# Gated product kernel (x times y through tanh-GELU): two DRAM stretches in place of three, the first x load in four row groups

## The chip, the cores and the metric

The kernel runs on one core of a Trainium2 chip. The metric is the device time of one execution in microseconds; three runs of the kernel before gave a median of 119.74 us.

## The reference

```python
def setup_inputs():
    batch, dim = 1024, 4096
    return {
        "x": np.random.randn(batch, dim).astype(np.float32),
        "y": np.random.randn(batch, dim).astype(np.float32),
    }

def reference(x, y):
    z = x * y
    return (0.5 * z * (1 + np.tanh(np.sqrt(2 / np.pi) * (z + 0.044715 * z ** 3)))).astype(np.float32)
```

Everything is elementwise in float32. Each input and the output have 1024 x 4096 elements, 16.78 MB.

## The kernel before

Since nothing depends on an element's place, the kernel is free in how it lays the data out. It takes each array as one flat run of 128 x 32768 elements and cuts it into contiguous DRAM stretches (PIECES, L14). In each stretch, row p of 128 equal rows goes to SBUF partition p (`columns`, L51 to L55). The three stretches have rows of 1280, 16384 and 15104 elements, that is 5,120, 65,536 and 60,416 bytes. All of x (32768 columns, `xs`) stays in SBUF; the product and the GELU are written over it, and the stores read it. y goes through a smaller buffer, `ys`, of 20440 columns, so later parts of y overwrite earlier ones.

The work is ordered by hand:

- SP's queue (q1 in the profile) and ACT's queue (q10) both issue DMAs. `_hoist` (L25) moves an instruction to the program's very beginning, ahead of the opening barrier. The small x piece (on SP, L79) and the large second x piece (on ACT, L80) are hoisted.
- SP then waits for the small x piece (L81), loads y's first part (columns 1280 to 17664) and x's third piece (L82, L83). It loads y's other parts as the buffer comes free: the second after three products, the last, small one after four (Y_FREE, L18; loop L84 to L87).
- VectorE (DVE) multiplies in steps (STEPS, L20: four of 4096 columns, seven of 2048, one of 768, one of 1280), ahead of each part waiting for its x and y (L94, L95). ACT waits for each product (L105) and applies the GELU in place (L106). `sem_mul` and `sem_act` count products and activations.
- SP stores the three stretches (L111 to L115). The first store waits for y's second part to have landed (L113) besides its own activations; the small stretch is stored last. Then SP waits for the stores and clears the semaphores.

Each DMA adds 16 to its semaphore when all of it has landed. One row of a DMA is one packet in the trace; the core has 16 DMA engines, and a DMA of 128 rows gives each engine eight.

Of the kernel before, what the change touches and what calls it, by code (L numbers as in the profile page):

```python
# [1 line left out]

# [4 lines left out]


F32 = mybir.dt.float32
GELU = mybir.ActivationFunctionType.Gelu_apprx_tanh  # L10

PIECES = [(0, 1280), (1280, 17664), (17664, 32768)]  # L14

Y_LOADS = [(1280, 17664, 4056), (17664, 32768, 0), (0, 1280, 15104)]

Y_FREE = [0, 3, 4]  # L18

STEPS = [[4096] * 4, [2048] * 7 + [768], [1280]]  # L20
STORES = [(1280, 17664), (17664, 32768), (0, 1280)]
Y_BUF = 20440


def _hoist(nc, issued):  # L25

    here = nc.cur_bb.bb.instructions
    first = nc.main_func.blocks[0].instructions
    for ins in issued:
        del here[next(k for k, i in enumerate(here) if i is ins or i.name == ins.name)]  # L30
    engine = issued[0].engine
    at = next(
        k
        for k, i in enumerate(first)
        if i.engine == engine and type(i).__name__ == "InstDrain"
    )
    first[at:at] = issued


@with_exitstack  # L40
def kernel(
    ctx: ExitStack,
    tc: tile.TileContext,
    x: bass.AP,
    y: bass.AP,
    out: bass.AP,
):
    nc = tc.nc
    P = nc.NUM_PARTITIONS

    def columns(t, a, b):  # L51

        flat = t.flatten_outer_dims().rearrange("r c -> (r c)")
        pa, pb = next(q for q in PIECES if q[0] <= a and b <= q[1])
        return flat[P * pa : P * pb].rearrange("(p c) -> p c", p=P)[:, a - pa : b - pa]  # L55


    tc.close()
    tc.compile()  # L59

    xs = nc.alloc_sbuf_tensor("xs", [P, PIECES[-1][1]], F32).ap()
    ys = nc.alloc_sbuf_tensor("ys", [P, Y_BUF], F32).ap()
    sem_x = [nc.alloc_semaphore(f"sem_x{i}") for i in range(len(PIECES))]
    sem_y = [nc.alloc_semaphore(f"sem_y{i}") for i in range(len(Y_LOADS))]
    sem_mul = nc.alloc_semaphore("sem_mul")
    sem_act = nc.alloc_semaphore("sem_act")
    sem_o = [nc.alloc_semaphore(f"sem_o{i}") for i in range(len(STORES))]

    def load_x(i, engine=nc.sync):
        a, b = PIECES[i]  # L70
        return engine.dma_start(out=xs[:, a:b], in_=columns(x, a, b)).then_inc(sem_x[i], 16)

    def load_y(i):
        a, b, r = Y_LOADS[i]
        return nc.sync.dma_start(
            out=ys[:, r : r + b - a], in_=columns(y, a, b)
        ).then_inc(sem_y[i], 16)

    _hoist(nc, [load_x(0).ins])  # L79
    _hoist(nc, [load_x(1, nc.scalar).ins])  # L80
    nc.sync.wait_ge(sem_x[0], 16)  # L81
    load_y(0)  # L82
    load_x(2)  # L83
    for i in range(1, len(Y_LOADS)):  # L84
        if Y_FREE[i]:
            nc.sync.wait_ge(sem_mul, Y_FREE[i])
        load_y(i)  # L87

    n = 0
    done = {}  # L90
    for i, (a, b, r) in enumerate(Y_LOADS):
        for j, (xa, xb) in enumerate(PIECES):
            if xa <= a < xb:
                nc.vector.wait_ge(sem_x[j], 16)  # L94
        nc.vector.wait_ge(sem_y[i], 16)  # L95
        c = a
        for w in STEPS[i]:
            nc.vector.tensor_mul(  # L98
                out=xs[:, c : c + w],
                in0=xs[:, c : c + w],  # L100
                in1=ys[:, r + c - a : r + c - a + w],
            ).then_inc(sem_mul, 1)
            n += 1
            done[c + w] = n
            nc.scalar.wait_ge(sem_mul, n)  # L105
            nc.scalar.activation(  # L106
                out=xs[:, c : c + w], in_=xs[:, c : c + w], func=GELU
            ).then_inc(sem_act, 1)
            c += w

    for i, (a, b) in enumerate(STORES):  # L111
        if i == 0:
            nc.sync.wait_ge(sem_y[-2], 16)  # L113
        nc.sync.wait_ge(sem_act, done[b])
        nc.sync.dma_start(out=columns(out, a, b), in_=xs[:, a:b]).then_inc(sem_o[i], 16)  # L115
    for i in range(len(STORES) - 1):
        nc.sync.wait_ge(sem_o[i], 16)
    nums = sorted(s.num for s in [*sem_x, *sem_y, *sem_o[:-1], sem_mul, sem_act])
    assert nums == list(range(nums[0], nums[-1] + 1))
    nc.sync.sem_clear(range(nums[0], nums[-1] + 1))  # L120
    nc.sync.wait_ge(sem_o[-1], 16).then_inc(sem_o[-1], -16)


# [1 line left out]
_INS = ['x', 'y']  # L125
_OUTS = [((1024, 4096), 'float32')]


# [23 lines left out]
```

## Time and profile before

| | |
|---|---|
| runs, median (lowest, highest) | 119.74 us (119.72, 119.80) |
| span of the profiled execution | 118.52 us |
| the median less that span | 1.22 us |
| VectorE busy | 35.2 us (30%), 13 products |
| ScalarE (ACT) busy | 31.0 us (26%), 13 activations and a table load |
| HBM read, written | 33.55 MB, 16.78 MB |

The profiled execution has no time of its own beside its span; the 1.22 us are what the runs have around a span of this length. "Issue to landing" in the DMA table runs from the issuing instruction to the last arrival at the semaphore, so it holds the time that a transfer queued behind others. The strips divide the span, or the window asked for, into 40 equal slices; a digit is the busy share in tenths.

The SP queue issued its DMAs at 0.00 (small x), 13.57 (y, first part), 13.96 (x, third piece), 55.78 (y, second part), 60.12 (y, last part), 78.27, 96.55 and 97.71 us (the stores); ACT's queue issued its load at 0.13.

### The profile page before, as it was taken

What the parts mean: (1) busy time and instruction counts of PE and PEld (TensorE: products, weight loads), DVE (VectorE), ACT (ScalarE), POOL (GpSimd) and SP (SyncE); (2) the same over time, 40 slices, a digit from 0 to 9 for tenths busy, and PEclk for the clock granted to TensorE, in tenths of its full rate; (3) what the DMA queues carried; (4) which work ended last, traced back from release to release, by engine and by line L of the source; (5) the groups of instructions that cost most, each with busy time, mean ns of one, the idle gap of its engine ahead of it and who ended that gap; (6) DMA issues with size and microseconds to landing.
All of it is one profiled execution on the core that took longest, in us unless ns stands there. A gap on an engine that the chain in (4) does not pass through costs nothing.

```text
span 118.5 us, 82 instructions
## 1 busy us (share of the span) xinstructions
DVE 35.2 (30%) x13; ACT 31.0 (26%) x14; POOL 0.2 (0%) x4
## 2 busy tenths in 40 slices
DVE  0000000000000069999920000059999940000000
ACT  4000000000000000977975000006998990000000
POOL 0000000000000000000000000000000000000000
DMA  9888899889988897797797797798899887977975
GB/s 492 382 382 382 354 575 487 354 354 398 664 354 354 354 652 326 326 652 326 326 632 347 326 632 347 326 575 354 354 531 531 354 354 326 652 326 326 652 326 221
DMA packets 1296, 50.33 MB, mean 425 GB/s; under 512 B 144, under 2 KB 144, under 8 KB 528
## 3 DMA queue, kind: packets, MB, share of 16 engines
q1 hardware_dynamic: 1152, 41.94, 82.2%
q10 hardware_dynamic: 144, 8.39, 16.5%
HBM read 33.55 MB, written 16.78 MB: 425 GB/s over the span
## 4 chain that ended last, share of the span: by engine, by line
DMA 55%; DVE 24%; ACT 3%; issue 1%; DVEq 0%
DMA ys<-in_y_dram 43%; DVE xs L98 24%; DMA xs<-in_x_dram 11%; ACT xs L106 3%; DVEq L95 0%
## 5 line engine op out<-in xcount | busy, mean ns | idle before, releaser
L98 DVE TENSOR_TENSOR xs<-xs,ys 128x2048 f32<-128x2048 f32 (+3 forms) x13 | 35.2, 2777 | 60.9 <-DMA ys<-in_y_dram 60.9
L106 ACT ACTIVATE xs<-xs 128x2048 f32<-128x2048 f32 (+3 forms) x13 | 29.7, 2301 | 65.1 <-DVE xs L98 65.1
L106 ACT ACT_TABLE_LOAD x1 | 1.3, 1283 | 1.6 <-PEq L59 1.6
L136 POOL MEMSET const-bfloat16-1.0<- 128x1 bf16 x1 | 0.1, 103 | 0.0
L136 POOL MEMSET const-uint8-127<- 128x1 uint8 x1 | 0.1, 102 | 0.0
L136 POOL MEMSET const-float32-0.0<- 128x1 f32 x1 | 0.1, 100 | 0.2 <-issue 0.2
L136 POOL MEMSET const-float32-1.0<- 128x1 f32 x1 | 0.1, 99 | 0.0
## 6 DMA issues: line engine op xcount, KB each, us to landing
xs<-in_x_dram SPq DMA_DIRECT2D x1, 7552.0 KB, 46.5
ys<-in_y_dram SPq DMA_DIRECT2D x1, 7552.0 KB, 22.5
out_dram<-xs SPq DMA_DIRECT2D x1, 7552.0 KB, 20.4
xs<-in_x_dram SPq DMA_DIRECT2D x1, 640.0 KB, 13.6
ys<-in_y_dram SPq DMA_DIRECT2D x1, 640.0 KB, 19.7
out_dram<-xs SPq DMA_DIRECT2D x1, 640.0 KB, 20.8
xs<-in_x_dram ACTq DMA_DIRECT2D x1, 30.4
ys<-in_y_dram SPq DMA_DIRECT2D x1, 29.0
```

What stands on the lines that cost most here:

```text
L98: nc.vector.tensor_mul(out=xs[:, c : c + w], in0=xs[:, c : c + w], in1=ys[:, r + c - a : r + c - a + w],).then_inc(sem_mul, 1)
L106: nc.scalar.activation(out=xs[:, c : c + w], in_=xs[:, c : c + w], func=GELU).then_inc(sem_act, 1)
L136: nc = _bacc.Bacc("TRN2", target_bir_lowering=False, num_devices=1)
```

## The change

There are two stretches (HALVES) of 15872 and 16896 elements a row, 63,488 and 67,584 bytes. The small piece is gone.

- x's first stretch is loaded by four DMAs of 32 rows each: group g takes partitions g, g + 4, g + 8 and so on. All add to one semaphore, and VectorE waits for 64 on it. Group 0 is hoisted on SP. The other groups and x's whole second stretch follow on SP with no wait between them. The rows of the second stretch are longer than 64 KB and are issued as 128 x 2 x 8448 elements.
- The hoisted DMA on ACT's queue is now y's first part (15872 columns) instead of x's large piece.
- y's second stretch is loaded in two parts of 12800 and 4096 columns, 51,200 and 16,384 bytes of each row, after three and after four products.
- Products and activations have new steps: three of 4096 and one of 3584 columns; five of 2048 and one of 2560; then 2048, 1280 and 768.
- There are two stores. The first waits for the four activations of its stretch and for the fifth product, which is the first on y's second part; the second waits for all activations.

```diff
-PIECES = [(0, 1280), (1280, 17664), (17664, 32768)]
+HALF = 15872
+HALVES = [(0, HALF), (HALF, 32768)]
 
-Y_LOADS = [(1280, 17664, 4056), (17664, 32768, 0), (0, 1280, 15104)]
+GROUPS = 4
 
-Y_FREE = [0, 3, 4]
-
-STEPS = [[4096] * 4, [2048] * 7 + [768], [1280]]
-STORES = [(1280, 17664), (17664, 32768), (0, 1280)]
+Y_LOADS = [(0, 15872, 4568, 0), (15872, 28672, 0, 3), (28672, 32768, 12800, 4)]
+STEPS = [[4096] * 3 + [3584], [2048] * 5 + [2560], [2048, 1280, 768]]
 Y_BUF = 20440
...
-    def load_x(i, engine=nc.sync):
-        a, b = PIECES[i]
-        return engine.dma_start(out=xs[:, a:b], in_=columns(x, a, b)).then_inc(sem_x[i], 16)
+    def load_group(g):
+        return nc.sync.dma_start(
+            out=xs[g::GROUPS, :HALF], in_=columns(x, 0, HALF)[g::GROUPS]
+        ).then_inc(sem_x[0], 16)
...
-    _hoist(nc, [load_x(0).ins])
-    _hoist(nc, [load_x(1, nc.scalar).ins])
-    nc.sync.wait_ge(sem_x[0], 16)
-    load_y(0)
-    load_x(2)
+    _hoist(nc, [load_group(0).ins])
+    _hoist(nc, [load_y(0, nc.scalar).ins])
+    for g in range(1, GROUPS):
+        load_group(g)
+    a, b = HALVES[1]
+    nc.sync.dma_start(out=xs[:, a:b], in_=columns(x, a, b)).then_inc(sem_x[1], 16)
     for i in range(1, len(Y_LOADS)):
-        if Y_FREE[i]:
-            nc.sync.wait_ge(sem_mul, Y_FREE[i])
+        nc.sync.wait_ge(sem_mul, Y_LOADS[i][3])
         load_y(i)
...
-    for i, (a, b) in enumerate(STORES):
-        if i == 0:
-            nc.sync.wait_ge(sem_y[-2], 16)
-        nc.sync.wait_ge(sem_act, done[b])
+    first = len(STEPS[0])
+    nc.sync.wait_ge(sem_act, first)
+    nc.sync.wait_ge(sem_mul, first + 1)
+    for i, done in enumerate((first, n)):
+        a, b = HALVES[i]
+        nc.sync.wait_ge(sem_act, done)
         nc.sync.dma_start(out=columns(out, a, b), in_=xs[:, a:b]).then_inc(sem_o[i], 16)
```

More of the change, by code (lines that the diff above doesn't have):

```diff
@@ L53, in columns @@
         flat = t.flatten_outer_dims().rearrange("r c -> (r c)")
-        pa, pb = next(q for q in PIECES if q[0] <= a and b <= q[1])
-        return flat[P * pa : P * pb].rearrange("(p c) -> p c", p=P)[:, a - pa : b - pa]
+        ha, hb = next(h for h in HALVES if h[0] <= a and b <= h[1])
+        return flat[P * ha : P * hb].rearrange("(p c) -> p c", p=P)[:, a - ha : b - ha]
     tc.close()
     tc.compile()
-    xs = nc.alloc_sbuf_tensor("xs", [P, PIECES[-1][1]], F32).ap()
+    xs = nc.alloc_sbuf_tensor("xs", [P, HALVES[-1][1]], F32).ap()
     ys = nc.alloc_sbuf_tensor("ys", [P, Y_BUF], F32).ap()
-    sem_x = [nc.alloc_semaphore(f"sem_x{i}") for i in range(len(PIECES))]
+    sem_x = [nc.alloc_semaphore(f"sem_x{i}") for i in range(2)]
     sem_y = [nc.alloc_semaphore(f"sem_y{i}") for i in range(len(Y_LOADS))]
@@ L66, with load_y @@
     sem_act = nc.alloc_semaphore("sem_act")
-    sem_o = [nc.alloc_semaphore(f"sem_o{i}") for i in range(len(STORES))]
-    def load_x(i, engine=nc.sync):
-        a, b = PIECES[i]
-        return engine.dma_start(out=xs[:, a:b], in_=columns(x, a, b)).then_inc(sem_x[i], 16)
-    def load_y(i):
-        a, b, r = Y_LOADS[i]
-        return nc.sync.dma_start(
+    sem_o = [nc.alloc_semaphore(f"sem_o{i}") for i in range(2)]
+    def load_group(g):
+        return nc.sync.dma_start(
+            out=xs[g::GROUPS, :HALF], in_=columns(x, 0, HALF)[g::GROUPS]
+        ).then_inc(sem_x[0], 16)
+    def load_y(i, engine=nc.sync):
+        a, b, r, _ = Y_LOADS[i]
+        return engine.dma_start(
             out=ys[:, r : r + b - a], in_=columns(y, a, b)
         ).then_inc(sem_y[i], 16)
-    _hoist(nc, [load_x(0).ins])
-    _hoist(nc, [load_x(1, nc.scalar).ins])
-    nc.sync.wait_ge(sem_x[0], 16)
-    load_y(0)
-    load_x(2)
+    _hoist(nc, [load_group(0).ins])
[4 more added lines that the diff above has]
+    nc.sync.dma_start(out=xs[:, a:b], in_=columns(x, a, b)).then_inc(sem_x[1], 16)
     for i in range(1, len(Y_LOADS)):
-        if Y_FREE[i]:
-            nc.sync.wait_ge(sem_mul, Y_FREE[i])
+        nc.sync.wait_ge(sem_mul, Y_LOADS[i][3])
         load_y(i)
     n = 0
[L90 to L94, printed above, removed]
+    for i, (a, b, r, _) in enumerate(Y_LOADS):
+        if i == 0:
+            nc.vector.wait_ge(sem_x[0], 16 * GROUPS)
+        if i == 1:
+            nc.vector.wait_ge(sem_x[1], 16)
         nc.vector.wait_ge(sem_y[i], 16)
@@ L103 @@
             n += 1
-            done[c + w] = n
             nc.scalar.wait_ge(sem_mul, n)
@@ L109 @@
             c += w
-    for i, (a, b) in enumerate(STORES):
-        if i == 0:
-            nc.sync.wait_ge(sem_y[-2], 16)
-        nc.sync.wait_ge(sem_act, done[b])
+    first = len(STEPS[0])
[4 more added lines that the diff above has]
+        nc.sync.wait_ge(sem_act, done)
         nc.sync.dma_start(out=columns(out, a, b), in_=xs[:, a:b]).then_inc(sem_o[i], 16)
-    for i in range(len(STORES) - 1):
-        nc.sync.wait_ge(sem_o[i], 16)
-    nums = sorted(s.num for s in [*sem_x, *sem_y, *sem_o[:-1], sem_mul, sem_act])
+    nc.sync.wait_ge(sem_o[0], 16)
+    nums = sorted(s.num for s in [*sem_x, *sem_y, sem_o[0], sem_mul, sem_act])
     assert nums == list(range(nums[0], nums[-1] + 1))
     nc.sync.sem_clear(range(nums[0], nums[-1] + 1))
-    nc.sync.wait_ge(sem_o[-1], 16).then_inc(sem_o[-1], -16)
+    nc.sync.wait_ge(sem_o[1], 16).then_inc(sem_o[1], -16)
 _INS = ['x', 'y']
```

## The prediction

> **What bounds the kernel now.** Read first: the page's strip and queue table; then the chain of waits; then the DMA view in narrow windows; last the trace's records of single DMA packets (one for each row that a DMA engine moves).
>
> ```profile
> span 118.5 us, 82 instructions
> ...
> DMA  9888899889988897797797797798899887977975
> ...
> q1 hardware_dynamic: 1152, 41.94, 82.2%
> q10 hardware_dynamic: 144, 8.39, 16.5%
> HBM read 33.55 MB, written 16.78 MB: 425 GB/s over the span
> ```
>
> The packets fill 82.2 + 16.5 = 98.7% of the sixteen engines' span. Idle are 1.3% of 118.5, about 1.5 us, and 1.0 of these lies ahead of the first packet. The chain of waits seems to say something else:
>
> ```profile
> 13.57 28.99 DMA ys<-in_y_dram
> ...
> 42.66 13.11 DVE xs L98 x3
> ...
> 55.78 22.47 DMA ys<-in_y_dram
> ...
> 80.56 13.30 DVE xs L98 x6
> ```
>
> It gives VectorE 13 us from 42.66. But it only follows semaphores back: the y load issued at 55.78 queued behind an x load that landed later:
>
> ```profile
> xs<-in_x_dram SPq DMA_DIRECT2D x1, 7552.0 KB, 46.5
> ys<-in_y_dram SPq DMA_DIRECT2D x1, 7552.0 KB, 22.5
> out_dram<-xs SPq DMA_DIRECT2D x1, 7552.0 KB, 20.4
> xs<-in_x_dram SPq DMA_DIRECT2D x1, 640.0 KB, 13.6
> ys<-in_y_dram SPq DMA_DIRECT2D x1, 640.0 KB, 19.7
> out_dram<-xs SPq DMA_DIRECT2D x1, 640.0 KB, 20.8
> ```
>
> That x load was issued at 13.96 and landed at 13.96 + 46.5 = 60.4. The y load behind it landed at 55.78 + 22.5 = 78.25. So the queue held work all the time, and compute is hidden. The same rows give the pace: an engine moved 8 rows of 60,416 B in 78.25 - 60.4 = 17.84 us, or 36.9 ps per byte; the small store's rows took (118.49 - 116.98)/8 = 0.189 us for 5,120 B, also 36.9. Time is bytes, plus what is lost at the start and in gaps. Two windows show those losses (40 slices each, 0.0 to 4.0 and 78 to 80 us; a packet is booked in the slice in which it starts, so zeros after the long rows have started are no idleness):
>
> ```profile
> DMA  0000000000995375796979799990000000000000
> ```
>
> ```profile
> DMA  9974997799499749950752999909000000000000
> ```
>
> In the first, nothing moves for 1.0 us, then 5 KB rows come in unevenly. In the second, the digits 0, 7, 5, 2 between 78.9 and 79.1 are engines that have finished the last y rows while the store's first rows, issued at 78.27, start at 79.11.
>
> **The change part by part.** Every byte still moves once. Per engine: before, 48 loaded and 24 stored rows; after, loads are 8 (x groups) + 8 (y) + 16 (x's second stretch, each row in two pieces of 33,792 B) + 8 + 8 = 48, stores 8 + 16 = 24. Bytes and row count equal: 0. Bounds: no row of 33,792 B is in this trace. The 5,120 B stores have packet starts 196.6 ns apart where 36.95 ps per byte make 189, 7 ns more. If the half rows alone cost that: 32 x 7 ns = 0.22 less the 0.06 of the 8 small stores given up, +0.17. If only the small ones cost it, -0.06. I take 0, being nearer to 60,416 B rows, which keep to the pace.
>
> *Start.* On average the engines are done with what x's first two pieces and y's first load hold (8 x 5,120 + 16 x 65,536 B, 40.18 us at 36.87 ps) at 41.87, a loss of 1.69. Following the packet records engine by engine splits it: the first packets begin between 1.01 and 1.61, mean 1.20; slow 5 KB rows cost 24 x (0.210 - 0.196) = 0.34 an engine, of which 0.23 are first rows (mean excess, the worst 0.756 against 0.196); the first 64 KB rows of ACT's queue cost 8 x (2.438 - 2.418) = 0.16. After, the hoisted DMA has 32 rows instead of 128, two for each engine if they spread evenly. With a quarter of the rows I give the ramp a quarter of its 0.6 us: mean start 1.08. First-row delay (0.23) and ACT queue's (0.16) stay, the 0.11 of later small rows goes: 1.47, so -0.22. Bounds: no delay beyond 1.01 at all, -0.68; each engine with the worst first row (+0.56), the worst ACT row (2.682 against 2.418, +0.26) and today's mean start: 2.02, +0.33. I take -0.22, since it keeps each row that has a counterpart.
>
> SP issues five more DMAs in a row (three groups, x's second stretch; the wait for x's first piece at L81 is gone), 0.4 us each as at L71: from about 1.6 to 3.2. The first group's two rows alternate with y's rows and last four times 2.34 us, to 10.4: cover 7 us. Without it, each late issue would cost its 0.4.
>
> *Middle.* x's first half and y's first load are 16 rows of 63,488 B; against before that is 73,728 B less, 2.72 us, and 0.22 of start: landed at 42.56 - 2.94 = 39.6. Three products of 4096 columns (13.1) let SP pass its wait at 52.8 for y's second part; the fourth (3.8) at 56.6 for the third. Behind these waits in SP's queue stand only the later y load and the stores. x's second stretch streams until 39.6 + 16 x 1.247 = 59.55, so y's second part is 59.55 - 52.8 - 0.85 = 5.9 us early (0.85: the store's issue at 78.27 to first packet 79.11). No gap. Were it later than that, every microsecond would count in full.
>
> *The gap at 79.* Mean end of the last y rows 79.08 by the records, mean first store packet 79.19: 0.11 lost, up to 0.31 on single engines. After, y's second part lands at 59.55 + 8 x 51,200 x 36.9 ps = 74.66; one product (2.29 + 0.1) and the issue pass to 77.05; store rows are ready at 77.9. The 16 KB rows of y last until 74.3 + 4.84 = 79.15 on the latest engine and 78.6 on the earliest, so they cover the new wait on the fifth product by 0.7. The gap closes: -0.11 (0 if the late engines set the end anyway; -0.31 if the most delayed does). If that cover were gone, each microsecond by which the product is late would stand in the span.
>
> *End.* The remaining products (four of 2.22, then 2.75, 2.22, 1.41, 0.87 by 1.05 ns a column) end at 93.2, the last ACTIVATE (0.83) at 94.1. The second store is ready by 95, the first streams to about 97.9: hidden by 3 us. One store less and one load semaphore more are single 9 ns packets: 0.
>
> Sum: 118.52 - 0.22 - 0.11 = 118.19. Runs have a median of 119.74, 1.22 above the profiled span; I keep that: 119.41, so 119.4.
>
> One rule stands against it. Every DMA of before has 128 rows; none shows 32. The Trainium skill, "DMA: Bandwidth & Descriptors", "Rules for kernel authors", says that peak rate wants 128 partitions in a DMA and that one 128-partition transfer beats split ones. "SBUF — State Buffer", section on the DMA port swizzle, explains it by ports, four neighbouring partitions to a port and the same port again 32 further on; rows 0, 4, 8 and so on reach all sixteen, but which engine gets which row no page says for 32 rows. If two engines met at one port and shared its rate, x's rows would take twice as long and the sum would be 138; if not, it stays 119.4.
>
> **The rivals.**
>
> *The start pays the same.* Lost time at the start could be latency that a long first row pays like a short one, and a start near 1.2. For it: 0.23 are first rows, and 64 KB rows are slow at first too. Against it: 0.6 us of ramp under 128 rows. Then only the gap is gained, or not even that: 119.6 to 119.7, no difference.
>
> *The row groups run slower.* Place: the first 39 us, where an engine moves 8 x rows of 2.34 us = 18.7. For it: no 32-row DMA is in the trace, and its slowest kind of row, 5,120 B, was 7% over its own best on average (0.210 for 0.196). Against: long rows keep 2.42 in either queue. At 7%: 119.74 + 1.31 - 0.33 = 120.7; at twice the time, the far end, 138. It decides from 0.33/18.7 = 1.8%, and from 3.0% it is a measurable loss.
>
> *The half rows are slow.* x's second stretch and the second store are 32 packets of 33,792 B in 40 us. Priced as the 5,120 B stores are (196.6 ns, 38.4 ps a byte), they cost 32 x 33,792 x 1.5 ps = 1.6 more: 119.4 + 1.6 = 121.0. Against it: the 7 ns look like a price per row, not per byte.
>
> *The change misses its cover.* The fifth product comes after y's last rows are through; it has 0.7 us to spare, and the product would have to be later by more. At 1 us late the gap is 0.3 and the time 119.7; at 1.5 us late, 120.2.
>
> **How the numbers follow.** About 0.2%, 0.24 us, is what a measurement of this kernel can tell from no change: below 119.50 is faster, above 119.98 slower. Forecast 0.47; equal start 0.22 (same); row groups 0.19; half rows 0.09; missed cover 0.03, counted half as same, half as slower. Faster 0.47, same 0.23, slower 0.30. The forecast's own terms reach from 119.74 - 0.68 - 0.31 - 0.06 = 118.7 to 119.74 + 0.33 + 0.17 = 120.2; both low ends together are unlikely, so I cut the range at 118.9, and carry it up to 120.8 over the 7% case. Left out are the half rows at full price and heavier group losses, about 0.17, and little below.
>
> **What would show it.** Right: sixteen engines' first packets within 0.2 us after 1.0; x rows of 2.34 us in all groups; first x and y landed by 39.6; no thin slices between 78 and 80; last landing near 118.1. Wrong: x rows in the groups above 2.40 us, half rows above 1.26, a thin strip before 39 or around 59, SP still issuing the groups when an engine runs dry, or VectorE's fifth product later than 78.

## The result and the profile after

The changed kernel takes 120.33 us (four runs, 120.23 to 120.69) against 119.73 for the kernel before in the same comparison (119.71 to 119.80). The ratio is 1.0052, interval 1.0039 to 1.0066: half a per cent slower, where the forecast was 0.3 per cent faster. The profiled execution took 120.37 us with a span of 119.02, so 1.35 lie around the span. (A second profile of the kernel before, further down, has 119.89 and 118.56, so 1.33. The 1.22 of the prediction set one run's span against other runs' median.)

The page of the changed kernel: span, strip, queues, and DMAs from issue to landing.

```profile
span 119.0 us, 81 instructions
...
DMA  9799779978987899998989696997997799898994
...
q1 hardware_dynamic: 1168, 42.21, 82.1%
q10 hardware_dynamic: 144, 8.13, 16.3%
HBM read 33.55 MB, written 16.78 MB: 423 GB/s over the span
...
xs<-in_x_dram SPq DMA_DIRECT2D x1, 8448.0 KB, 56.7
out_dram<-xs SPq DMA_DIRECT2D x1, 8448.0 KB, 23.5
xs<-in_x_dram SPq DMA_DIRECT2D x4, 1984.0 KB, 28.9
ys<-in_y_dram ACTq DMA_DIRECT2D x1, 7936.0 KB, 35.5
```

The kernel is as DMA-bound as before: the two queues' packets fill 82.1 + 16.3 = 98.4% of the engines' span. So the loss must be a matter of tenths in one place, and the narrow windows find it. First the DMA view from 0.0 to 4.0 us in slices of 0.1 us (a packet is booked where it starts):

```profile
DMA  0000000000099999000000000000000000000009
GB/s 0 0 0 0 0 0 0 0 0 0 0 3809 1905 1270 1905 1270 0 0 0 0 0 0 0 0 0 0 0 0 0 0 0 0 0 0 0 0 0 0 0 635
DMA packets 17, 1.08 MB, mean 270 GB/s; under 512 B 0, under 2 KB 0, under 8 KB 0
```

Sixteen rows start between 1.1 and 1.6 us, all 63,488 B long and all of ACT's queue, which this view lists alone with 16 packets. Only one more row starts before 4.0, though such a row takes 2.34 us and the next should have started from 3.5 on. Then the timeline of the first stretch:

```profile
0.00 0.54 SPq L67 DMA_DIRECT2D xs<-in_x_dram  x1
0.12 0.38 ACTq L73 DMA_DIRECT2D ys<-in_y_dram  x1
```

The 32-row DMA holds SP for 0.54 us, the 128-row one holds ACT for 0.38: y's rows came first, x's group second. And the DMA view from 78 to 80 us:

```profile
DMA  9977077797077909077099090999990999000900
```

Here rows of y and, from 79.1, of the store start at scattered times, so single zeros are no idleness; the packet records show no engine idle for more than 0.01 us there. The gap has closed as forecast.

**Where the loss sits.** The packet records give for each DMA the sixteen small packets with which the engines report its end. I took the latest of the sixteen engines at two points. "Start's loss": when it has moved the first x and y loads, less its bytes at 36.87 ps each. "Rest": from there, with the start's bytes put back, to its last packet. Before: 42.19 - 40.17 = 2.02, and 118.11 - 2.02 = 116.09; after: 39.96 - 37.45 = 2.51.

```
                                            first-row excess  start's loss  rest     end
kernel before                               0.23              2.02          116.09   118.11
kernel before, second profile               0.19              2.05          116.11   118.16
changed kernel                              0.65              2.51          116.06   118.57
```

"First-row excess" is how much longer an engine's very first row took than a later one of its size, mean of sixteen; times in us. The rest agrees within 0.05 us although it holds all the half rows, the new waits, the closed gap and one store less. The start costs 0.49 us more, and the end comes 0.46 later: the whole difference is there when the first x and y have landed. On average over the sixteen engines the start's loss is 1.70 before, as the prediction had it, and 2.02 after.

### The profile page after: what moved, and what is told of

Read it like the earlier page. It is cut to its first block, busy times and chain, and to the rows that moved or that the text cites. A ratio compares the mean times of both kernels' runs of the same rounds, so it can differ in the third digit from the quotient of the medians.

```text
span 119.0 us, 81 instructions
## 1 busy us (share of the span) xinstructions
DVE 35.2 (30%) x13; ACT 30.9 (26%) x14; POOL 0.2 (0%) x4
## 3 DMA queue, kind: packets, MB, share of 16 engines
q1 hardware_dynamic: 1168, 42.21, 82.1%
q10 hardware_dynamic: 144, 8.13, 16.3%
## 4 chain that ended last, share of the span: by engine, by line
DMA 50%; DVE 23%; ACT 5%; SPq 1%; issue 0%; DVEq 0%
DMA xs<-in_x_dram 31%; DVE xs L96 23%; DMA ys<-in_y_dram 18%; ACT xs L103 5%; SPq L67 1%; DVEq L93 0%
## 5 line engine op out<-in xcount | busy, mean ns | idle before, releaser
L96 DVE TENSOR_TENSOR xs<-xs,ys 128x2048 f32<-128x2048 f32 (+5 forms) x13 | 35.2, 2779 | 58.7 <-DMA xs<-in_x_dram 40.3
L103 ACT ACTIVATE xs<-xs 128x2048 f32<-128x2048 f32 (+5 forms) x13 | 29.6, 2302 | 62.7 <-DVE xs L96 62.7
## 6 DMA issues: line engine op xcount, KB each, us to landing
ys<-in_y_dram SPq DMA_DIRECT2D x1, 2048.0 KB, 23.1
```

The lines of the kernel that those rows point to most:

```text
L96: nc.vector.tensor_mul(out=xs[:, c : c + w], in0=xs[:, c : c + w], in1=ys[:, r + c - a : r + c - a + w],).then_inc(sem_mul, 1)
L103: nc.scalar.activation(out=xs[:, c : c + w], in_=xs[:, c : c + w], func=GELU).then_inc(sem_act, 1)
```

## The experiments

Each ratio is against the kernel before in the same comparison (119.82 to 119.91 us there).

**The start, first round.** Four edits of the changed kernel.

One DMA of 128 rows in place of the groups:

```diff
-GROUPS = 4
+GROUPS = 1
```

> x's first stretch in one hoisted DMA of 128 rows instead of four of 32; all else as in the changed kernel. In its profile the sixteen engines begin with y rows of ACT's queue (1.13 to 1.59 us) and each engine's first 63,488 B row takes 2.95 us on average where a later one takes 2.34, an excess of 0.61. Theory A (the strided 32-row DMA takes longer to be set up, 0.54 us at its issue against 0.38, so x comes second and the start is late): SP's x rows begin at about 1.0 again, first-row excess about 0.25, time 119.7 to 119.9. Theory B (any long row that is the first on its engine pays, whichever queue it is from): first-row excess 0.5 to 0.7 again, time 120.2 to 120.4.

120.45 us, ratio 1.0043 (1.0031 to 1.0055). Its DMA view from 0.0 to 4.0 us:

```profile
DMA  0000000009999900999000000000000000000009
GB/s 0 0 0 0 0 0 0 0 0 635 4444 1905 635 635 0 0 635 635 635 0 0 0 0 0 0 0 0 0 0 0 0 0 0 0 0 0 0 0 0 635
```

x's rows begin at 1.0, as theory A wants, and still take 3.09 us as first rows, an excess of 0.75. A is wrong: neither the groups nor the order of the queues is the cause. B had the mechanism, with excess and time slightly above its ranges. (For the changed kernel the records give 2.99 and an excess of 0.65, not the 2.95 and 0.61 of the expectation.)

Columns instead of rows, the hoisted DMA with 5,120 B rows that begin 63,488 B apart:

```diff
-GROUPS = 4
+GROUPS = 2
+CUTS = [0, 1280, HALF]
...
-            out=xs[g::GROUPS, :HALF], in_=columns(x, 0, HALF)[g::GROUPS]
+            out=xs[:, CUTS[g] : CUTS[g + 1]], in_=columns(x, CUTS[g], CUTS[g + 1])
```

> x's first stretch split by columns instead of by rows: the hoisted DMA takes 128 rows of 5,120 B, the next the other 58,368 B of each row. Both A and B: the start is that of the kernel before (first packets from 1.0, mean loss at the start 1.7 instead of 1.98, latest engine 0.49 earlier), time 119.7 to 119.9. If instead the loss comes from the two stretches, the half rows or the new waits, it stays at 120.2 to 120.4.

120.28 us, ratio 1.0032 (1.0020 to 1.0044): between the two cases. The profile, of the fastest of its runs (120.06 us), has a start's loss of 2.15 and a rest of 116.11. Its 5 KB first rows paid 0.53 us, twice as much as in the kernel before, where they lie end to end.

SP waiting for group 0 ahead of the other groups, and ACT's load not hoisted:

```diff
+    nc.sync.wait_ge(sem_x[0], 16)
     for g in range(1, GROUPS):
```

> SP waits for group 0 to have landed (about 14 us) ahead of the other three groups and x's second stretch, as the kernel before waited for its small piece. Theory C (the four DMAs that SP issues from 1.8 to 4.2 us, while the first rows are under way, slow those): first-row excess falls from 0.61 to 0.3 or less, time 119.8 to 120.0. Theories A and B: excess stays at about 0.6, time 120.2 to 120.5. The y rows cover the wait in every theory.

```diff
-    _hoist(nc, [load_y(0, nc.scalar).ins])
+    load_y(0, nc.scalar)
```

> y's first load is issued on ACT behind the opening barrier (about 1.8 us) instead of ahead of it, so the engines must begin with group 0 of x. Theory A: the group's rows begin late (1.3 us or more) though nothing is ahead of them, first-row excess about 0.25. Theory B: they begin at about 1.0 to 1.2 and pay 0.5 to 0.7. Time in A 120.0 to 120.4, in B 120.1 to 120.4; here the first packets decide, not the time.

The first took 120.66 us (1.0063, 1.0049 to 1.0076) with an excess of 0.70, a little above the range given: DMAs issued meanwhile do not slow the first rows, and theory C is wrong. The second took 120.75 us (1.0073, 1.0061 to 1.0085), more than either theory gave. With nothing ahead of it, the group's first packets come at 1.33 us or later, as A said of the set-up, but the excess is 0.80, even above B's 0.5 to 0.7. The strided 32-row DMA is slow to start; in the changed kernel y's rows, from 1.13 us on, fill the engines meanwhile.

**Place in DRAM, the gap, the second half.** The kernel before with the first piece inside a longer stretch:

```diff
+DRAM = [(0, 17664), (17664, 32768)]
...
-        pa, pb = next(q for q in PIECES if q[0] <= a and b <= q[1])
+        pa, pb = next(q for q in DRAM if q[0] <= a and b <= q[1])
```

> The kernel before with one thing changed: its small first piece lies inside a stretch of 17664 columns, so the hoisted DMA reads its 5,120 B rows 70,656 B apart instead of end to end. All DMAs keep their sizes and order. Theory D (rows that begin far apart in DRAM cost the first packets more: in the run by columns the same 5 KB rows, 63,488 B apart, paid 0.53 us as first packets and 0.67 an engine in all, against 0.23 and 0.34 in the kernel before): first-row excess about 0.5, latest engine 0.2 to 0.4 later, time 0.2 to 0.4 above before. Theory B (only the length of the first row counts): as before within 0.1.

120.13 us, ratio 1.0021 (1.0013 to 1.0030), excess 0.51, start's loss 2.21, rest 116.12. So a start with 5 KB rows that lie apart cost 0.2 us more than one with rows end to end. The edit did a little more than its expectation says: x's large piece, y's first and last parts and two of the stores lie at the wider pitch too. But the rest is as before, so nothing behind the start paid for it; which of the first loads' pitches counts is not separated.

The kernel before without the wait that makes its gap:

```diff
-        if i == 0:
-            nc.sync.wait_ge(sem_y[-2], 16)
```

> The kernel before without the wait for y's landing ahead of the first store (L113), so the store's rows stand behind y's last rows early and the gap at 79 us closes. If the gap costs the end what the prediction gave it: 0.1 us less than before. Theory S (the latest engine has no gap and alone sets the end; the gap only lets the early ones fall back): the latest engine's end unchanged, spread of the engines at the end 0.5 instead of 0.17 us, time as before within 0.05.

Neither: 121.04 us, ratio 1.0096 (1.0083 to 1.0109). The start is as before (1.98), the rest 117.16. Where y's last 5 KB rows should be through by 79.1, the DMA view from 78 to 80 us is thin to its end:

```profile
DMA  9592909626699098699929299589590429793499
DMA packets 94, 0.48 MB, mean 241 GB/s; under 512 B 0, under 2 KB 0, under 8 KB 94
```

Hardly an engine is idle, but 241 GB/s: the small rows took 2.5 us instead of 1.5, with the store's rows waiting behind them. The run can't say what the gap costs, because the early store costs ten times as much. An answer comes from the rest in profiles whose later rows ran at pace: 116.09, 116.11 and 116.12 with the gap, 116.06, 116.11 and 116.11 without (changed kernel, one group, columns). These kernels differ in more than the gap, but to the engine that ends last it is worth 0.05 us at most.

The changed kernel with the kernel before's hoisted DMA (a contiguous stretch of its own for 1280 columns, with a load of y and a store of its own):

```diff
+CUT = 1280
+DRAM = [(0, CUT), (CUT, HALF), (HALF, 32768)]
...
-GROUPS = 4
+GROUPS = 2
...
-            out=xs[g::GROUPS, :HALF], in_=columns(x, 0, HALF)[g::GROUPS]
+            out=xs[:, DRAM[g][0] : DRAM[g][1]], in_=columns(x, *DRAM[g])
```

> The changed kernel with x's first 1280 columns (and y's and the output's) in a contiguous stretch of their own: the hoisted DMA is that of the kernel before, the row groups are gone, and all from x's second stretch on is as changed; y's small piece is a load of its own on SP behind x's. Theories B and D: start as in the kernel before, time 0.0 to 0.15 above before. If something behind the start costs (half rows, the second y parts, the waits): 0.4 to 0.6 above before, as the changed kernel.

120.28 us, ratio 1.0033 (1.0020 to 1.0045): not the 0.0 to 0.15 expected. Excess 0.27, as in the kernel before, but a start's loss of 2.46 on the latest engine, much of it one engine whose first long row took 0.63 us too long, and a rest of 116.18. On average over the engines the start's loss is 1.81, near the kernel before's 1.70. It moves 96 rows an engine instead of 72, 24 of them small; eight of these lie in the rest, and at the prediction's 7 ns each that is an estimated 0.06 of the 0.1 there.

Rows of 1,280 B in the run by columns (`CUTS = [0, 320, HALF]`):

> The run by columns with a hoisted DMA of 320 columns: 128 rows of 1,280 B, 63,488 B apart. Theory D: first-row excess still about 0.5, time as in the run by columns or above (0.3 to 0.5 over before). Theory B: excess clearly smaller than 0.5, and y's long rows, which then start while the chip is still cold, pay instead; time 0.2 to 0.5 over before.

120.54 us, 0.63 above before and so above both forecasts; ratio 1.0052 (1.0039 to 1.0066), start's loss 2.72. The very first rows paid 0.16 on average, but later ones of the small rows up to 1.16: each engine met several delays. Shorter rows alone do not help; B as "length only" is too simple.

**Which array, which wait.** The kernel before with ACT's and SP's first large loads exchanged:

```diff
-    _hoist(nc, [load_x(1, nc.scalar).ins])
+    _hoist(nc, [load_y(0, nc.scalar).ins])
...
-    load_y(0)
+    load_x(1)
```

> The kernel before with ACT's hoisted load and SP's later one exchanged: ACT loads y's first part, SP x's large piece, sizes unchanged. Theory T (two arrays cold at once cost the start more than one): latest engine 0.2 to 0.4 later, time 0.2 to 0.4 above before. Otherwise within 0.1 of before.

119.90 us, ratio 1.0006 (0.9998 to 1.0015). Two arrays at once cost nothing: theory T is wrong. (Its profile is of the slowest of its runs, 120.39 us.) The like exchange in the run with a stretch of its own:

> The run with a stretch of its own for the first 1280 columns (0.37 above before), with the same exchange the other way round: ACT loads the rest of x's first half, SP the rest of y's. Theory T: its loss goes, time 0.0 to 0.15 above before. Theory W (what is missing is the kernel before's wait on SP, which keeps further DMAs from being issued into the start): stays at 0.3 to 0.4.

120.18 us, ratio 1.0031 (1.0019 to 1.0043), start's loss 2.22 (1.78 on average), rest 116.40. It stays slow, which W allowed, but W falls with the next run, the kernel before without SP's first wait:

```diff
-    nc.sync.wait_ge(sem_x[0], 16)
```

> The kernel before without SP's wait for the small piece (L81), so that y's first part and x's third piece are issued from about 1.6 us. Theory W: time 0.2 to 0.5 above before, with the loss in the first 5 us. Theory T: within 0.1.

119.91 us, ratio 1.0005 (0.9996 to 1.0014), start's loss 2.14, rest 116.14: no difference.

A small piece of 2560 columns in the kernel before (PIECES cut at 2560 and 18944, y's parts and steps to match):

> The kernel before with a small piece of 2560 columns: hoisted rows of 10,240 B end to end, and 3 us of y's last rows to cover the first store's issue. Theory S: the gap at 79 closes, which is worth nothing to the latest engine. Theories B and D: the start as before or a little later (longer first rows, 1.3 MB touched instead of 0.65): time 0.0 to 0.2 above before. If the gap counted: 0.1 below.

120.43 us, ratio 1.0055 (1.0043 to 1.0067): 0.57 above before, where 0.0 to 0.2 was the most expected. Its 10 KB first rows paid 0.61 us, almost as much as long ones, but the engines that started first paid it and those that started late did not: these rows all ended between 2.06 and 2.35 us, and the start's loss is 1.98. So it is the latest engine's sum that counts, not the first rows' mean. The gap closed, and the rest is 116.72. The time went in the middle: y's second part was issued at 57.30, the loads ahead of it ended at 59.9, and y's first rows behind them were 0.15 to 0.32 us too long on eight engines; one engine lost 0.5 in these rows. A lead of 2.6 us did not keep the rows at pace; 3.9 us in the kernel before (55.78 to 59.7) did. That is read from one profile, not tried.

**Regions, and the start alone.** A kernel before whose long rows begin half a 64 KB off (first piece 1344 columns), and one whose second piece has 15872 columns (in both, y's parts, steps and stores are changed to match):

```diff
-PIECES = [(0, 1280), (1280, 17664), (17664, 32768)]
+PIECES = [(0, 1344), (1344, 17728), (17728, 32768)]
```

> The kernel before with a small piece of 1344 columns: the 65,536 B rows behind it keep their length but begin 688,128 B into the array, 10.5 times 65,536, instead of 655,360, ten times. Theory P (the first touch of each 64 KB region costs a delay, and a row that straddles two pays twice): latest engine 0.2 to 0.4 later at the start, time 0.2 to 0.4 above before. If P is wrong: within 0.1.

```diff
-PIECES = [(0, 1280), (1280, 17664), (17664, 32768)]
+PIECES = [(0, 1280), (1280, 17152), (17152, 32768)]
```

> The kernel before with its second piece of 15872 columns, so that ACT's first rows are 63,488 B as in the changed kernel; small piece, waits and gap unchanged. Theory P: 0.2 to 0.4 above before. If only the length and order of the first rows count: within 0.1.

119.87 us (1.0007, 0.9998 to 1.0015) and 119.92 us (1.0007, 0.9998 to 1.0015), start's losses 1.99 and 1.96. Theory P is wrong, and 62 KB rows are as good as 64 KB ones behind short rows. The changed kernel with stretches of 16384 columns (y's parts and steps to match) agrees:

```diff
-HALF = 15872
+HALF = 16384
```

> The changed kernel with both stretches of 16384 columns: rows of exactly 65,536 B at multiples of 65,536, row groups kept. Theory P: first rows' mean excess falls from 0.65 to 0.45 or less, time 0.2 to 0.4 above before instead of 0.6. If P is wrong: excess 0.6 to 0.8, time 0.5 to 0.7 above before.

120.34 us, ratio 1.0045 (1.0029 to 1.0061), excess 0.71, start's loss 2.41. This run has no half rows either, as x's second stretch moves in rows of 65,536 B, and it is still slow. And the second profile of the kernel before:

> The kernel before, unchanged: a second profile of it. If the start's loss is a property of the kernel, its latest engine is again 1.9 to 2.2 us behind its bytes at the end of the first loads and the span again 116.1 more than that; if one lucky profile stood in the comparison, it is 2.4 or more.

119.85 us, ratio 0.9996 (0.9986 to 1.0006); its row is in the table above. The small loss at the start is no luck of one profile.

The kernel before with long rows first, its small piece no longer hoisted:

```diff
-    _hoist(nc, [load_x(0).ins])
+    load_x(0)
```

> The kernel before with its small piece no longer hoisted, so that the engines' first rows are ACT's 65,536 B rows; small piece, sizes, gap and tail stay. Theory B (an engine whose first row is long loses its whole first delay, and the engines lose unequally): first-row excess 0.6 to 0.8, latest engine 0.4 to 0.6 later, time 0.4 to 0.6 above before, with nothing of the changed kernel's second half in it. If the change's second half is what costs: within 0.1 of before.

122.83 us, ratio 1.0246 (1.0232 to 1.0260), far more than expected, because the edit did two things. The excess of the first rows is 0.72, as B said, with none of the change's second half there. When both hoisted loads were in, at 23.28 us, the latest engine had moved 8 x 65,536 + 8 x 5,120 B, 20.84 us at 36.87 ps each: a loss of 2.44, 0.42 above the kernel before's 2.02 and within B's forecast of 0.4 to 0.6. But the small piece then landed late, SP's wait for it held the next loads back, and the queue ran dry. The DMA view from 21 to 26 us (slices of 0.125 us):

```profile
DMA  0000000000368641100000000000999909000000
GB/s 0 0 0 0 0 0 0 0 41 41 123 287 328 246 164 41 41 0 0 0 0 0 0 0 0 0 0 0 2097 3146 2097 524 0 524 0 0 0 0 0 0
```

From 23.1 to 24.5 nothing starts; the engines are idle for 1.85 us on average. What was not foreseen is behind it: y's first rows after this pause took 0.83 us too long on average, up to 1.20. The same rows in the kernel before, at 15.1 us behind running loads, took 0.003 too long. So the delay does not belong to the first microseconds of the program. In both places it met long loads that started on engines with nothing under way.

The changed kernel without the wait for its fifth product:

```diff
-    nc.sync.wait_ge(sem_mul, first + 1)
```

> The changed kernel without the wait for the fifth product ahead of its first store, which is then issued at about 61 us behind y's last loads. In the kernel before the like removal cost 1.1 us, all of it in y's last rows. If that is a matter of the 5 KB rows there, nothing is lost here (0.5 to 0.7 above before, as the changed kernel); if stores queued behind loads slow any of them, 1.2 to 2 us above before.

121.92 us, ratio 1.0179 (1.0156 to 1.0202), 2.1 us above before. The profile, of its fastest run, has 0.83 us more in y's last rows, 16,384 B each, on the latest engine (5.70 instead of 4.87). So a store queued early behind loads slowed these loads here too, with longer rows, and the wait that the change kept is worth over a microsecond by the runs' medians.

## Why the prediction was wrong

**Bounds of the kernel: right.** DMA engines stay busy, compute stays hidden. Products start at 40.3 (forecast 39.6), the fifth is done at 77.9 (77.05), the last activation at 95.5 (94.1). Two slips did not enter the sum: behind the hoisted one SP issues four more DMAs, not five (0.47 to 0.60 us each, not 0.4), and the small store's rows are 0.197 us apart by the records, as the prediction itself says further down, not 0.189.

**Rows: right.** Half rows of x's second stretch start 1.247 us apart on the latest engine (19.96 us for 16), as forecast, and the term is 0. The rival of slow half rows is excluded.

**The start: the step that failed.** The prediction said "First-row delay (0.23) and ACT queue's (0.16) stay", carrying the delay of a 5,120 B first row over to one of 63,488 B. It counted -0.22, a mean over the engines. Measured is 0.65 for the first row and a mean start at 1.30 instead of 1.08: by the mean the start costs 2.02 - 1.70 = +0.32, just inside the upper bound of +0.33, and for the engine that counts +0.49, outside it. That bound let the worst 5 KB row (0.56) stand for all long rows; single long ones lost 1.0. The runs show that all starts with long first rows lose 2.4 to 2.9 us on the latest engine (changed kernel 2.51; 2.60, 2.88, 2.68, 2.41 and 2.76 in its variants). Starts with 5 KB rows end to end, in the kernel before's layout, lose 1.96 to 2.14 (one with the queues exchanged, in the profile of its slowest run, 2.26). The kernel before with long rows first lost 2.44.

**The ramp: wrong.** A quarter of the rows did not give a quarter of the ramp. The 32-row DMA took longer to issue (0.54 against 0.38) and its rows came behind y's.

**The gap: mis-sized.** -0.11 was a mean over engines. The prediction named the right end of the bound, "0 if the late engines set the end anyway", and didn't take it; measured is a rest 0.03 shorter. From the end of the first loads on, the mean engine did gain: 36.91 ps a byte against 37.03, some 0.25 us over the rest. All of that fell to engines that were not last.

**The mean in place of the latest.** This is the second error, behind the gap and part of the start. By means, the changed kernel ends only 0.08 us later than before (118.09 against 118.02); by the latest engine 0.46 (118.57 against 118.11). The start spreads the engines by 0.85 us, and with no pause in the stream they keep that spread to the last packet. Of the 0.92 us between 119.41 and 120.33 the start makes 0.71, the gap and the rest 0.08; the remaining 0.13 is the time outside the packets, above all the 1.35 around the span that stood at 1.22.

**The rivals.** "The start pays the same" had the right place and too small a price. The row groups do not run slow: x's first rows take 2.37 us (one of them 2.54) and later ones 2.34, where the rival at its far end had 4.68. The Trainium skill ("DMA: Bandwidth & Descriptors", "Rules for kernel authors") advises one 128-partition transfer in place of two to disjoint partition halves. Here one DMA and four row groups stand within 0.1% of each other (1.0043 and 1.0052), so these runs show no price for such a split. The port rule of its page "SBUF — State Buffer" ("Door 1: The DMA port swizzle") was not put to the test, since by that rule each group reaches all sixteen ports.

**What stays open.** Long first rows on idle engines lose 0.65 to 0.80 us on average and end 0.5 to 1.1 us apart; 5 KB rows end to end lose 0.2 to 0.4, far apart 0.5. That is shown, for long rows also at 24.6 us. What makes the delay is not. Also open is why the two runs with a contiguous 5 KB start in front of the changed second half stayed 0.3% slow. Their mean start's loss (1.81 and 1.78) is near the kernel before's 1.70, so the short start did help; but in the first run one engine fell 0.6 us behind in one row, and in the second the rest is 0.3 longer with no row after 5 us more than 0.1 us late. So giving the changed kernel back the old start did not give back the old time. No run here beat the kernel before.

## What to carry to other kernels

Where the DMA engines were always busy, as here, the span was the loss at the start of the engine that is latest, plus its bytes: reckon with that engine, not with the mean. The best starts here had first rows that were short and end to end in memory, so that the first delays were paid on small rows and the long rows found their engine running; try that first, though it did not rescue the changed kernel. Hold stores back until the loads ahead of them are nearly through: both kernels lost over a microsecond without that wait. A load issued 3.9 us or more ahead of need kept its first rows at pace, and one issued 2.6 us ahead did not; the latter is one profile.

## What the runs showed of the hardware

- Long loads on idle engines lose 0.65 to 0.83 us on average, at 1 us and again at 24.6 us after a pause; stores after the short pause at 79 us (0.11 us on average) lost only 0.03.
- Stores queued behind loads slowed these loads: 1.1 us for 5 KB rows in the kernel before, about 1.5 us in the changed one with 16 KB rows (ratio 1.0179 against 1.0052; 0.83 us of it in these rows in the profile of the fastest run).
- A DMA of 32 rows with a step of four partitions held its queue longer (0.47 to 0.60 us) than a hoisted one of 128 rows (0.38) and brought its first packet later (1.33 against 1.00 us). Whether the step or the number of rows does it was not tried.
- Engines kept the spread that they had, 0.85 us from 4 us to the last packet in the changed kernel. In the kernel before the pause at 79 us levelled them, from 0.49 to 0.18.
